# The page table as one 64-byte row per partition, pool_scale on GpSimd's queue, and the new tokens' pooling output kept in SBUF

## The chip, the cores and the metric

The kernel runs on one core of one Trainium2 chip. The metric is the device time of one execution in microseconds (us). An engine is called here by the name that the profile gives it: PE (TensorE's matmuls), PEld (its weight loads), DVE (VectorE), ACT (ScalarE), POOL (GpSimd) and SP (SyncE, which here only issues transfers). A `q` behind an engine's name means its instruction queue, where transfers are issued.

## The reference: what is computed

One step of a decoder layer for 1024 new prompt tokens and, for each of 8 samples, one new token behind 256 cached ones. All is float32.

```
p = rmsnorm(x) @ w_in          # split: q | cmp kv | slc kv | win kv | gates | za | u | zp
attn = gated sum of three branches (compressed blocks, selected blocks, window of 512)
pool = pool_mixer(u) * pool_scale          # 4 groups of 128 channels, windows 2, 4, 8, 16
y    = rmsnorm(x + concat(attn * silu(za), pool * silu(zp)) @ w_out)
cached keys and values of a sample: cache[page_table[sample]]     # 8 x 2 pages of 128 tokens
```

The page table has 8 x 2 int32 numbers, 64 bytes in all. `pool_scale` has 512 floats.

## The kernel before, in words

Every large product is made of three float32r products of high and low parts, so that each weight tile is first split: ACT copies the raw tile into a high part (`split_w`, L139), and DVE or POOL subtracts it for the low part (L140). The program runs in these stages.

1. The prompt's rows are normalised and transposed into `x` (chunks of 384 tokens), while the first token-major product (compressed keys and values, `cmp_unit`) already runs. SP loads `x_t` and the weights `w_raw`.
2. Two more token-major products, over selected and over window keys and values (loop over `br`, L302 to L339). A unit is 128 tokens: 24 matmuls (L244 to L246) into one of two PSUM banks, then on ACT a copy `kvf` (L314) and a copy into `V` (L316), on DVE the low part of `V` (L317). The keys are then transposed on PE (`kp`, L324). On PE the transpose of unit t stands behind the matmuls of unit t+1, and it reads `kvf` of unit t.
3. Queries, compression of keys and values (with cached pages fetched by indirect DMA through `idx`), pooling groups (`u`, `zp`), with the new tokens' attention (`decode`) in between.
4. Attention over the prompt in 32 units, with the `za` gates, the output weights and the output projection as filler.

Instruction order: inside stage 1 the order on ACT, DVE, PE and POOL is that of the code. From L301 on, the framework orders the instructions of each engine at build time, so a small change of the code can move other instructions too. Every engine then runs its list in order: an instruction that waits holds back all behind it on its engine.

The weights of stage 3 (`ws_raw`, `load_tile`, L348) have two buffers. The first of them, for the queries, are loaded and split during stage 2: SP issues them behind the last `w_raw`, and ACT's splits (L139) stand in ACT's list between the `kvf` copies of stage 2.

Three places are touched by the change.

- The page table: `pti` is loaded on SP by two DMAs, one for each half of the partitions. Each of 64 partitions takes 8 numbers with a stride of two, so 1024 runs of 4 bytes in all. POOL turns them into row indices (`ptf` L384, `idx` L386), which the indirect DMAs of stage 3 read.
```
for h in range(2):
    nc.sync.dma_start(pti[h * 64:(h + 1) * 64], dap(ptab, h, [[0, 64], [2, NB], [1, 1]]))
```
- `psc` (L669), `pool_scale` laid out with one channel per partition and four groups: 512 runs of 4 bytes, on SP's queue behind the last query weights; DVE halves it (L670). The pooling output (L812, L816) reads it.
- The pooling output `bb` goes to DRAM (`b_d`, L818) and comes back in stage 4 as `mb` (`split_m`, L966), one tile of tokens at a time. The ninth tile holds the 8 new tokens. It is `m8` in the output projection (L999).

Of the kernel before, what the change touches and what calls it, by code (L numbers as in the profile page):

```python
# [7 lines left out]
F32 = mybir.dt.float32  # L8
F32R = mybir.dt.float32r
I32 = mybir.dt.int32  # L10
# [11 lines left out]
NEG = -1.0e9  # L22
# pacing of the filling products: steps per block of attention (gate path, output), blocks added per unit,
# steps at the start, lag in products
NZ, NO, C0, OW, PLAG = 0.8, 0.5, 2, 12, 100
ZORD = ([(0, 0), (0, 1), (0, 2), (1, 0), (1, 1), (1, 2)]
        + [(pt, c) for c in range(3) for pt in (2, 3)])
# the rows of the output weights, by half of their columns, that take the place of each chunk of x
WROWS = [[(0, k) for k in (4, 5, 6, 7, 0, 1)], [(0, 2), (0, 3)] + [(1, k) for k in (4, 5, 6, 7)],
# [12 lines left out]
def hybrid_step_kernel(ctx, tc, xp, xs, ccmp, cslc, cwin, spool, ptab, norm_g, w_in, cmp_pe, cmp_w1,  # L42
# [33 lines left out]

    # DRAM scratch
    q_d = dram.tile([2, 512, T], F32, name="q_d")
# [3 lines left out]

    # constants
    ident = pers.tile([128, 128], F32, name="ident")
# [7 lines left out]
    def ptr_rms(pool, ssq, n, name):  # L92
        """(ssq / D + eps) ** -0.5 for a [n, 1] column."""
        st = pool.tile([128, 2], F32, name=name, tag="rms", bufs=4)
        nc.gpsimd.tensor_scalar(st[:n, 0:1], ssq, 1.0 / D, 1e-6, op0=OP.mult, op1=OP.add)
        nc.gpsimd.tensor_tensor(st[:n, 1:2], st[:n, 0:1], mhalf[:n], op=OP.pow)
        return st[:n, 1:2]

    # persistent data
    KT = pers.tile([128, 2, KLEN], F32R, name="KT")  # L100
# [3 lines left out]
    qs_t = pers.tile([128, 4, NB], F32, name="qs_t")  # L104
    as_t = pers.tile([128, 4, NB], F32, name="as_t")
    mslc = pers.tile([128, T], BF16, name="mslc")
    mwin = pers.tile([128, 640], BF16, name="mwin")
# [55 lines left out]
    load_x(3)  # L163
    nc.sync.dma_start(pe32, cmp_pe)
    def spread_g(h):
        """The norm's weights from the first partition to all."""
        cs = slice(h * 512, h * 512 + 512)
        p = ps_any()
        nc.tensor.matmul(p, ones, gb[0:1, cs], start=True, stop=True)
        if h:  # L170
            nc.scalar.activation(gb[:, cs], p, AF.Copy)
        else:
            nc.vector.tensor_copy(gb[:, cs], p)

    # masks
    nc.gpsimd.memset(mslc, 0.0)
# [10 lines left out]

    # normalised x, transposed, as high and low parts
    rss = {}
# [35 lines left out]

    # token-major projections: compressed, selected and window keys and values, gate logits
    def tok_unit(hi, lo, cn, t, mid=None):
# [112 lines left out]
    nc.gpsimd.dma_start(g_d[:, :], gates[:NB, 8, :])  # L340
    # a token before the end of the first compressed block has no compressed branch
    vgate = pers.tile([128, 24], F32, name="vgate")
# [27 lines left out]
    def silu2(out, src):  # L370
        """2 * silu(src)"""
        nc.scalar.activation(out, src, AF.Tanh, scale=0.5)
        nc.vector.scalar_tensor_tensor(out, out, 1.0, src, op0=OP.add, op1=OP.mult)

    # page indices: row of 2 tokens each
    pti = keep.tile([128, NB], I32, name="pti")
    for h in range(2):
        nc.sync.dma_start(pti[h * 64:(h + 1) * 64], dap(ptab, h, [[0, 64], [2, NB], [1, 1]]))
    pm = keep.tile([128, 1], F32, name="pm")
# [3 lines left out]
    ptf = keep.tile([128, NB], F32, name="ptf")  # L383
    nc.gpsimd.tensor_copy(ptf, pti)  # L384
    idx = pers.tile([128, NB], I32, name="idx")
    nc.gpsimd.tensor_scalar(idx, ptf, 64.0, pm, op0=OP.mult, op1=OP.add)  # L386

    # compressed keys and values, prompt and samples
    ces = ExitStack()
# [98 lines left out]

    # queries
    for pt in range(4):  # L490
# [18 lines left out]
    def decode():  # L509
        """One new token per sample."""  # L510
        dp = des.enter_context(tc.tile_pool(name="dp", bufs=1, reuse_waits="tile"))
        # queries, one column per head and sample; qx: high parts, then low parts, per sample
        qs = dp.tile([128, NB, 8], F32, name="qs")
# [6 lines left out]
        def diag(ap):  # L520
            """The columns of each sample's own heads in [b, 2, 64] columns: [p, b, h]."""
            return bass.AP(tensor=ap.tensor, offset=ap.offset, ap=[ap.ap[0], [136, NB], [1, 8]])
# [59 lines left out]
        for br in range(2):  # L582
# [6 lines left out]
            for b in range(0, NB, 2):  # L589
# [8 lines left out]
                for bb in range(2):  # L598
                    f = dp.tile([128, 512], F32, name="kvx", bufs=4)
                    if br == 0:  # L600
                        nc.gpsimd.indirect_dma_start(out=f, out_offset=None, in_=cslc,
                                                     in_offset=bass.IndirectOffsetOnAxis(
                                                         ap=idx[:, b + bb:b + bb + 1], axis=0))
                    else:
                        nc.gpsimd.dma_start(f, cwin[b + bb].rearrange("(p two) c -> p (two c)", two=2))
                    for par in range(2):
                        nc.tensor.transpose(p[:, (bb * 2 + par) * 128:(bb * 2 + par + 1) * 128],
                                            f[:, par * 256:par * 256 + 128], ident)
                    # high and low parts of the values
                    v = dp.tile([128, 2, 2, 128], F32R, name="vx", bufs=8)  # L610
                    fv = f.rearrange("p (two f c) -> p two f c", two=2, f=2)[:, :, 1]
                    nc.scalar.activation(v[:, :, 0], fv, AF.Copy)
                    nc.gpsimd.tensor_sub(v[:, :, 1], fv, r32(v[:, :, 0]))
                    vx.append(v)
# [52 lines left out]
    bb = pp.tile([128, TOK], F32, name="bb")  # L667
    psc = pp.tile([128, 4], F32, name="psc")
    nc.sync.dma_start(psc, pool_scale.rearrange("(g p) -> p g", p=128))  # L669
    nc.vector.tensor_scalar(psc, psc, 0.5, None, op0=OP.mult)  # L670
    spt = pp.tile([120, 512], F32, name="spt")
# [11 lines left out]

    # pooling group
    at = ctx.enter_context(tc.tile_pool(name="at", bufs=2, reuse_waits="tile"))
# [16 lines left out]
    def stage1(i, pr_):  # L702
        """Scores and softmax of a pair of heads for 128 queries; yields between matmul groups."""
        kv = pr_ // 2
# [6 lines left out]
        sm = at.tile([128, 2, 4, 3], F32, name="sm", bufs=3)  # L711
        # the first tile of a head: compressed 0:64, selected 64:64+n; the second: window 0:wn
        c_m = mc[:, 56 - 8 * i:120 - 8 * i]
# [47 lines left out]
    for g in range(4):  # L761
# [44 lines left out]
        for c in range(3):  # L806
# [7 lines left out]
            else:  # L814
                # the last on the engine that stores them
                nc.scalar.activation(bb[:, cs], p[:, :n], AF.Copy, scale=psc[:, g:g + 1])  # L816
                nc.gpsimd.tensor_mul(bb[:, cs], bb[:, cs], sz[:, cs])
        nc.gpsimd.dma_start(b_d[g], bb)  # L818
    tc.keep_in_program_order(nc.sync.dma_start(npool_p, utok[:15]))
    tc.keep_in_program_order(nc.sync.dma_start(npool_s[:, 14], utoks))  # L820
    pes.close()

    # attention over the prompt; the gate path, the new tokens and the output projection fill in
    zap = ctx.enter_context(tc.tile_pool(name="zap", bufs=1, reuse_waits="tile"))
# [4 lines left out]
    def stage2(i, pr_):  # L829
        """Transposes, products with the values and their sum; a list of steps."""  # L830
        kv = pr_ // 2
# [63 lines left out]

    # tiles of za that hold one factor of the gated output: the gate or the attention's output
    half_done = set()
# [38 lines left out]
    def load_wo(c):  # L936
        """Output weights in the place of x's chunk c, which is no longer needed."""
        rows = WROWS[c]
# [20 lines left out]
    def split_m(i, part):  # L959
        """High and low parts of four of the eight row blocks of the mixed output."""  # L960
        op = O_["p"]
        t0 = i * 128
        n = 128 if i < 8 else NB
        if part:
            src = O_["p"].tile([128, 4, 128], F32, name="mb")[:, :, :n]
            nc.sync.dma_start(src, b_d[:, :, t0:t0 + n].rearrange("g p t -> p g t"))  # L966
        else:
            src = za[:, :, t0:t0 + n]
# [70 lines left out]
    def filler():  # L1039
# [7 lines left out]
        for i in range(1, 7):  # L1047
# [3 lines left out]
            for half in range(2):  # L1051
                yield from out_half(i, half, st)
        # the last tile: the pooling part ahead of its attention
        tail["r"] = load_r(7)
# [21 lines left out]
    def after(a, b):  # L1076
        """Keeps a behind b in their engine's order."""
        tc.add_manual_dep(a, b.name, mybir.DependencyInfo(
            mybir.DependencyClass.NoSync, mybir.DependencyReason.DATA), reason="order")

    def paced_fill(k):
        """Steps of the filler, none ahead of the attention's products emitted so far."""
        ins = nc.cur_bb.bb.instructions
# [121 lines left out]
```

## Time and profile before

| what | value |
|---|---|
| time, median of 3 runs | 656.16 us (655.71 to 656.98) |
| span of the profiled execution, first to last instruction | 654.4 us |
| median less span | 1.8 us |
| PE busy | 627.6 us, 96% of the span |
| PEld / DVE / ACT / POOL busy | 89% / 65% / 55% / 41% |
| mean granted TensorE clock | 0.990 |

The profiled execution is known by its span; the time of a run has also what lies around the span, so the two differ by 1.8 us. A busy share is an average over all stages, so the places where PE stands still are to be looked for one by one. In views of waits a line reads "who waited, on which tile, for whom". In a timeline the columns are start, length, engine, line, operation, and in brackets the idle time before it and what ended it; `x2` means that several instructions are merged. In a table of windows each engine has its busy time in the window, then come the granted clock as a share of 2.4 GHz, the share of the DMA engines' time that is busy, and GB/s.

### The profile page before, as it was taken

Reading aid. Unit: us, or ns where it says so; the run is one execution under the profiler, and the core shown is the slowest. Engines: PE = TensorE matmul, PEld = TensorE weight load, DVE = VectorE, ACT = ScalarE, POOL = GpSimd, SP = SyncE. Lnnn points to the kernel's source line nnn. Section 1 sums busy time; section 2 is a strip of 40 time slices with the busy share of each in tenths; the row PEclk is TensorE's granted clock in tenths of the full one; section 3 lists DMA queues with packets and bytes.
Section 4 is the critical chain, followed back from the end, with each engine's and each line's share of the span. In section 5 each row is a group of like instructions: output and inputs, shape, how many; then the busy total and the mean of one; then the engine's idle time right before and its main releaser. Section 6 shows DMA issues by size and latency. Waiting matters only on the chain. (4 is left out here: it accounts for less than half of the span.)

```text
span 654.4 us, 12214 instructions
## 1 busy us (share of the span) xinstructions
PE 627.6 (96%) x4141; PEld 581.6 (89%) x4141; DVE 426.0 (65%) x1306; ACT 361.0 (55%) x930; POOL 266.8 (41%) x410
## 2 busy tenths in 40 slices
PE   6995999999999999999999899999999999999995
PEld 4995999999999999998999888788899999988984
DVE  5741234555526547575797998779888788877652
ACT  5652233444413234325788787767587677665641
POOL 5153001431207424104565666736454445454511
PEclk9997999999999999999999999999999999999999
DMA  8432302984524342243313437212022030101001
GB/s 274 147 100 56 102 16 76 310 274 118 162 72 135 84 142 70 94 132 98 97 33 98 130 113 238 86 34 82 32 83 97 18 97 18 65 17 66 18 34 64
DMA packets 65677, 65.14 MB, mean 100 GB/s; under 512 B 6423, under 2 KB 56927, under 8 KB 65575
## 3 DMA queue, kind: packets, MB, share of 16 engines
q1 hardware_dynamic: 55599, 44.53, 22.8%
q0 software_dynamic: 3968, 12.76, 6.0%
q10 hardware_dynamic: 6048, 7.08, 3.0%
q8 instruction: 33, 0.54, 0.3%
q14 instruction: 29, 0.24, 0.1%
HBM read 50.99 MB, written 15.68 MB: 102 GB/s over the span
## 5 line engine op out<-in xcount | busy, mean ns | idle before, releaser
L756 POOL TENSOR_SCALAR Ps<-Ps,sm,gates 128x64 f32<-128x64 f32 (+1 forms) x120 | 75.3, 639 | 111.1 <-DVE sm L752 77.3
L736 PE MATMUL S<-KT,qt 128*128 128x320 f32 (+10 forms) x400 | 98.3, 347 | 1.9 <-DVE sm L699 1.8
L859 DVE TENSOR_TENSOR pl<-tp,ph 128x512 fp32r<-128x512 f32 (+1 forms) x136 | 89.9, 670 | 13.5 <-ACT ph L858 12.4
L858 ACT ACTIVATE ph<-tp 128x512 fp32r<-128x512 f32 (+1 forms) x136 | 76.6, 579 | 35.2 <-PE tp L853 28.2
L365 PE MATMUL pa<-x,ws_hi 128*128 128x384 f32 (+1 forms) x288 | 93.6, 325 | 0.0
L366 PE MATMUL pa<-x,ws_hi 128*128 128x384 f32 (+1 forms) x288 | 92.8, 322 | 0.0
L367 PE MATMUL pa<-x,ws_lo 128*128 128x384 f32 (+1 forms) x288 | 92.6, 322 | 0.0
L750 ACT ACTIVATE Ps<-Ps,sm 128x64 f32<-128x64 f32 (+8 forms) x128 | 70.6, 554 | 28.2 <-DVE sm L748 26.7
L995 PE MATMUL pj<-wo,mh 128*128 128x512 f32 x256 | 82.6, 400 | 0.0
L871 PE MATMUL O<-pl,V 128*128 128x256 f32 x264 | 77.7, 311 | 1.0 <-DVE pl L859 0.9
L870 PE MATMUL O<-ph,V 128*128 128x256 f32 x264 | 74.2, 295 | 0.0
L736 PEld LDWEIGHTS S<-KT,qt 128*128 128x128 f32 x400 | 63.9, 189 | 8.8 <-DVE sm L699 2.8
L244 PE MATMUL pa<-w_hi,x 128*128 128x256 f32 (+1 forms) x192 | 57.7, 301 | 0.2 <-DVE V L317 0.2
L246 PE MATMUL pa<-w_hi,x 128*128 128x256 f32 (+1 forms) x192 | 56.9, 296 | 0.4 <-DVE x L217 0.4
L245 PE MATMUL pa<-w_lo,x 128*128 128x256 f32 (+1 forms) x192 | 56.1, 293 | 0.0
L366 PEld LDWEIGHTS pa<-x,ws_hi 128*128 128x128 f32 x288 | 54.2, 188 | 0.4 <-issue 0.2
L365 PEld LDWEIGHTS pa<-x,ws_hi 128*128 128x128 f32 x288 | 54.2, 188 | 0.3 <-DVE us L776 0.2
L367 PEld LDWEIGHTS pa<-x,ws_lo 128*128 128x128 f32 x288 | 54.1, 188 | 0.3
L871 PEld LDWEIGHTS O<-pl,V 128*128 128x128 f32 x264 | 49.7, 188 | 4.8 <-DVE pl L859 3.0
L870 PEld LDWEIGHTS O<-ph,V 128*128 128x128 f32 x264 | 49.9, 189 | 2.0 <-ACT ph L858 0.2
L995 PEld LDWEIGHTS pj<-wo,mh 128*128 128x128 f32 x256 | 45.1, 188 | 7.0 <-PE S L736 0.4
L995 PE MATMUL pj<-wo,ml 128*128 128x512 f32 x128 | 50.6, 395 | 0.1
(279 smaller groups left out, 1530.9 us busy)
## 6 DMA issues: line engine op xcount, KB each, us to landing
ws_raw<-in_w_in SPq DMA_DIRECT2D x32, 256.0 KB
qt<-q_d SPq DMA_DIRECT2D x64, 128.0 KB
x_t<-in_x_prompt SPq DMA_DIRECT2D x8, 512.0 KB
wo_raw<-in_w_out SPq DMA_DIRECT2D x8, 512.0 KB
r<-in_x_prompt SPq DMA_DIRECT2D x8, 512.0 KB
out<-r SPq DMA_DIRECT2D x7, 512.0 KB
q_d<-qhl ACTq DMA_DIRECT2D x8, 384.0 KB
out<-kvf ACTq DMA_DIRECT2D x5, 512.0 KB
```

Source lines behind the costliest of these rows:

```text
L244: nc.tensor.matmul(p[:n, :cn], xh[c][:, k, ts_], hi[:, k, :cn], start=k == 0, stop=False)
L365: nc.tensor.matmul(p[:, :n], hi[:, k, :], xh[c][:, k, :], start=k == 0, stop=False)
L366: nc.tensor.matmul(p[:, :n], hi[:, k, :], xl[c][:, k, :], start=False, stop=False)
L367: nc.tensor.matmul(p[:, :n], lo[:, k, :], xh[c][:, k, :], start=False, stop=k == 7)
L736: nc.tensor.matmul(S[:, :ln], qt[:, f, h, :], KT[:, kv, k0 + a:k0 + a + ln], start=f == 0, stop=f == 1)
L750: nc.scalar.activation(regs[br], regs[br], AF.Exp, bias=sm[:, hh, 1, br:br + 1], accum_out=sm[:, hh, 2, br:br + 1])
L756: nc.gpsimd.tensor_scalar(regs[br], regs[br], sm[:, hh, 3, br:br + 1], gsrc[:, k:k + 1], op0=OP.mult, op1=OP.mult)
L858: nc.scalar.activation(ph[:, :m], tp[:, :m], AF.Copy)
L859: nc.vector.tensor_sub(pl[:, :m], tp[:, :m], r32(ph[:, :m]))
L870: nc.tensor.matmul(O[:, :256], vv, ph[:, a * 256:(a + 1) * 256], start=False, stop=False)
L871: nc.tensor.matmul(O[:, :256], vv, pl[:, a * 256:(a + 1) * 256], start=False, stop=last)
L995: nc.tensor.matmul(p, a[:, k % 4, :], w, start=first and kk == 0, stop=last and kk == 2)
```

## The change

`ptr` replaces `pti`: the 64 bytes of the page table go to each of 128 partitions in one DMA, issued on SP behind `pe32` in the first loads. POOL picks the numbers out with two copies. `psc` is loaded on POOL's queue at the end of stage 2 and halved on POOL. POOL copies the last 8 columns of each pooling output into `bs_t`, and the ninth tile of the output projection reads that in place of `mb`; its load is gone. Comments are removed as well, which shifts the line numbers.

```
+    bs_t = pers.tile([128, 4, NB], F32, name="bs_t")
+    psc = pers.tile([128, 4], F32, name="psc")
...
     nc.sync.dma_start(pe32, cmp_pe)
+    ptr = keep.tile([128, NB, 2], I32, name="ptr")
+    nc.sync.dma_start(ptr.rearrange("p b h -> p (b h)"), bc_rows(ptab, 128, 2 * NB))
...
     nc.gpsimd.dma_start(g_d[:, :], gates[:NB, 8, :])
+    nc.gpsimd.dma_start(psc, pool_scale.rearrange("(g p) -> p g", p=128))
+    nc.gpsimd.tensor_scalar(psc, psc, 0.5, None, op0=OP.mult)
...
-    pti = keep.tile([128, NB], I32, name="pti")
-    for h in range(2):
-        nc.sync.dma_start(pti[h * 64:(h + 1) * 64], dap(ptab, h, [[0, 64], [2, NB], [1, 1]]))
...
-    nc.gpsimd.tensor_copy(ptf, pti)
+    for h in range(2):
+        rs = slice(h * 64, h * 64 + 64)
+        nc.gpsimd.tensor_copy(ptf[rs], ptr[rs, :, h])
...
-    psc = pp.tile([128, 4], F32, name="psc")
-    nc.sync.dma_start(psc, pool_scale.rearrange("(g p) -> p g", p=128))
-    nc.vector.tensor_scalar(psc, psc, 0.5, None, op0=OP.mult)
...
                 nc.gpsimd.tensor_mul(bb[:, cs], bb[:, cs], sz[:, cs])
+                nc.gpsimd.tensor_copy(bs_t[:, g, :], bb[:, T:])
...
-        if part:
-            src = O_["p"].tile([128, 4, 128], F32, name="mb")[:, :, :n]
+        if part and i == 8:
+            src = bs_t
+        elif part:
+            src = O_["p"].tile([128, 4, 128], F32, name="mb")
```

Three places of the order show what this moves. First SP's queue from the first loads to the first weights of stage 3, before:

```order
L164 DMA pe_106<-in_cmp_pe 32x128
L148 DMA w_raw<-in_w_in 128x2x256 x2
L135 DMA x_t<-in_x_prompt 128x1024
L148 DMA w_raw<-in_w_in 128x2x256 x2
L135 DMA x_t<-in_x_prompt 128x1024 x3
L135 DMA x_t<-in_x_sample 8x1024
L148 DMA w_raw<-in_w_in 128x2x280 x4
L378 DMA pti<-in_page_table 64x8x1 x2
L354 DMA ws_raw<-in_w_in 128x4x128 x6
```

and of the change:

```order
L166 DMA pe_108<-in_cmp_pe 32x128
L168 DMA ptr<-in_page_table 128x16
L150 DMA w_raw<-in_w_in 128x2x256 x2
L137 DMA x_t<-in_x_prompt 128x1024
L150 DMA w_raw<-in_w_in 128x2x256 x2
L137 DMA x_t<-in_x_prompt 128x1024 x3
L137 DMA x_t<-in_x_sample 8x1024
L150 DMA w_raw<-in_w_in 128x2x280 x4
L360 DMA ws_raw<-in_w_in 128x4x128 x6
```

The page table has gone from the place between `w_raw` and `ws_raw` to the place behind `pe`, ahead of the second weights of stage 1.

Second POOL's list at the passage from stage 1 to stage 2 (`w_lo` of 128x560 are the window weights' low parts), before:

```order
L265 DMA out<-knew_11_612 8x256
L381 IOTA pm 64x1 x2
L140 TENSOR_TENSOR w_lo<-w_raw,w_hi 128x560 x2
L384 CAST ptf<-pti 128x8
L140 TENSOR_TENSOR w_lo<-w_raw,w_hi 128x560 x2
L386 TENSOR_SCALAR idx<-ptf,pm 128x8
L333 DMA out<-knew_20_900 8x256
```

and of the change:

```order
L269 DMA out<-knew_11_616 8x256
L345 DMA psc<-in_pool_scale 128x4x1
L384 IOTA pm 64x1 x2
L389 CAST ptf<-ptr 64x8 x2
L142 TENSOR_TENSOR w_lo<-w_raw,w_hi 128x560
L391 TENSOR_SCALAR idx<-ptf,pm 128x8
L142 TENSOR_TENSOR w_lo<-w_raw,w_hi 128x560 x2
L346 TENSOR_SCALAR psc<-psc 128x4
L142 TENSOR_TENSOR w_lo<-w_raw,w_hi 128x560
L337 DMA out<-knew_20_904 8x256
```

The load of `psc` has come in at the head, and the last of four `w_lo` now stands behind the halving of `psc`, which reads that load.

Third PE's list in the first part of `decode`, where a score product (`dS`) of the new tokens stands between the matmuls of a pooling group (`pa`), before:

```order
L365 MATMUL pa<-x_89,ws_hi 128x384
L366 MATMUL pa<-x_89,ws_hi 128x384
L367 MATMUL pa<-x_89,ws_lo 128x384
L621 MATMUL dS<-kxh,qx 128x258
L607 MATMUL dkt<-ident,kvx 128x128 x4
L622 MATMUL dS<-kxl,qx 128x258
L621 MATMUL dS<-kxh,qx 128x258
L622 MATMUL dS<-kxl,qx 128x258
L607 MATMUL dkt<-ident,kvx 128x128 x4
```

and of the change:

```order
L371 MATMUL pa<-x_91,ws_hi 128x384
L626 MATMUL dS<-kxh,qx 128x258
L612 MATMUL dkt<-ident,kvx 128x128 x4
L372 MATMUL pa<-x_91,ws_hi 128x384
L373 MATMUL pa<-x_91,ws_lo 128x384
L371 MATMUL pa<-x_91,ws_hi 128x384
L612 MATMUL dkt<-ident,kvx 128x128 x2
L372 MATMUL pa<-x_91,ws_hi 128x384
L373 MATMUL pa<-x_91,ws_lo 128x384
L627 MATMUL dS<-kxl,qx 128x258
L626 MATMUL dS<-kxh,qx 128x258
L627 MATMUL dS<-kxl,qx 128x258
```

Between the first transposes `dkt` and this first `dS` there were 34 matmuls `pa`, and there are 27 now; the group that stood together is spread. The rest of `decode` and stage 4 have shifts of the same kind. Up to `decode` the lists of PE, ACT and DVE have the same rows as before.

## Rows read from the trace of the kernel before

**Rows 1.** The page's head: span, and busy time of TensorE's two parts.

```profile
span 654.4 us, 12214 instructions
...
PE 627.6 (96%) x4141; PEld 581.6 (89%) x4141; DVE 426.0 (65%) x1306; ACT 361.0 (55%) x930; POOL 266.8 (41%) x410
```

**Rows 2.** Waits of PE, whole span: total, times, longest, in us.

```profile
PE kp L324 <- ACT kvf L314: 7.0, 1, 7.0
```

**Rows 3.** Timeline of PE in stage 2, around that wait.

```profile
54.30 0.28 PE L246 MATMUL pa<-w_hi,x 128*128 128x256 f32 x1
61.52 0.47 PE L324 MATMUL kp<-ident,kvf 128*128 128x128 f32 x1 [6.95 <-ACT kvf L314]
...
62.56 0.41 PE L245 MATMUL pa<-w_lo,x 128*128 128x256 f32 x1
62.77 0.41 PE L246 MATMUL pa<-w_hi,x 128*128 128x256 f32 x1
...
67.64 0.28 PE L244 MATMUL pa<-w_hi,x 128*128 128x256 f32 x1
67.76 0.28 PE L245 MATMUL pa<-w_lo,x 128*128 128x256 f32 x1
```

**Rows 4.** Timeline of ACT over the same stretch.

```profile
60.57 0.63 ACT L139 ACTIVATE ws_hi<-ws_raw 128x512 fp32r<-128x512 f32 x1 [9.96 <-DMA ws_raw<-in_w_in]
61.10 0.37 ACT L314 ACTIVATE kvf<-pa 128x256 f32<-128x256 f32 x1
...
64.77 0.63 ACT L139 ACTIVATE ws_hi<-ws_raw 128x512 fp32r<-128x512 f32 x1 [1.00 <-DMA ws_raw<-in_w_in]
```

**Rows 5.** Timeline of SP's queue: issues, in several narrow windows.

```profile
46.99 0.37 SPq L148 DMA_DIRECT2D w_raw<-in_w_in  x1
47.41 1.41 SPq L378 DMA_DIRECT2D pti<-in_page_table  x2
...
48.86 0.62 SPq L354 DMA_DIRECT2D ws_raw<-in_w_in  x1
...
61.95 0.37 SPq L354 DMA_DIRECT2D ws_raw<-in_w_in  x1
```

**Rows 6.** Windows: busy times, then clock, DMA share and GB/s.

```profile
49.50:55.00 5.50, 5.07 (x43) 4.87 (x42) 0.29 (x1) 1.11 (x2) 1.62 (x2) 1.00 0.05 2
...
57.40:67.60 10.20, 5.90 (x26) 5.61 (x27) 2.49 (x6) 3.40 (x8) 3.60 (x4) 0.50 0.40 99
```

**Rows 7.** Timeline of POOL over the same stretch.

```profile
48.38 2.74 POOL L140 TENSOR_TENSOR w_lo<-w_raw,w_hi 128x560 fp32r<-128x560 f32 x2
59.83 0.19 POOL L384 CAST ptf<-pti 128x8 f32<-128x8 int32 x1 [8.71 <-DMA pti<-in_page_table]
```

**Rows 8.** Timeline of PE: the first matmul that reads the window weights' low part.

```profile
81.55 0.29 PE L245 MATMUL pa<-w_lo,x 128*128 128x280 f32 x1
```

**Rows 9.** Instructions of tile psc: min/median/max ns, first and last start in us.

```profile
L669 SPq DMA_DIRECT2D psc<-in_pool_scale x1: 498/498/498, 191.4 to 191.4; - x1
L670 DVE TENSOR_SCALAR psc<-psc x1: 170/170/170, 196.5 to 196.5; 128x4 f32<-128x4 f32 x1
```

**Rows 10.** Timelines of DVE and PE at the first score product of decode.

```profile
221.68 0.14 DVE L596 TENSOR_TENSOR kxl<-kn,kxh 128x4 fp32r<-128x4 f32 x1
...
224.61 0.34 PE L367 MATMUL pa<-x,ws_lo 128*128 128x384 f32 x1
224.78 0.28 PE L621 MATMUL dS<-kxh,qx 128*128 128x258 f32 x1
```

**Rows 11.** Timelines of POOL and PE: the ninth tile's low part and its first use.

```profile
418.14 0.26 POOL L973 TENSOR_TENSOR m<-mb,m 128x32 fp32r<-128x32 f32 x1
...
423.65 0.71 PE L999 MATMUL pj<-wo,m 128*40 128x512 f32 x2
```

**Rows 12.** Windows over the rest of the program.

```profile
68.00:280.00 212.00, 212.00 (x1421) 206.05 (x1420) 105.43 (x265) 76.52 (x180) 57.10 (x78) 1.00 0.42 128
280.00:420.00 140.00, 134.87 (x899) 123.16 (x898) 109.55 (x452) 100.61 (x315) 79.48 (x136) 1.00 0.38 115
```

## The prediction

> **What bounds the kernel now.** I read the page's head first: PE is busy 627.6 of 654.4 us [rows 1], so a change can only help where PE stands still, or where it runs slowly. The view of waits of PE says where it stands still: the longest is 7.0 us in one piece, for the transpose `kp`, which wants `kvf` from ACT [rows 2]. The timeline puts it at the end of the third unit of stage 2: the last matmul starts at 54.30, and the transpose at 61.52, after 6.95 us of nothing [rows 3]. The reader should follow this wait back, engine by engine.
>
> On ACT, `kvf` ran at 61.10, directly behind a split `ws_hi` at 60.57, and that split had held ACT for 9.96 us, since 50.61, for the transfer of `ws_raw` [rows 4]. So ACT had nothing wrong with it: a weight tile that nobody needs before stage 3 stands in its list ahead of a copy that PE needs now. On SP's queue that `ws_raw` was issued at 48.86, directly behind the two loads of the page table at 47.41 [rows 5]. From issue to use it took 60.57 - 48.86 = 11.7 us. A `ws_raw` of the same shape, issued at 61.95, was in use at 64.77, so 2.8 us is what such a load takes when nothing is ahead of it [rows 4, 5]. What was ahead: POOL's copy of the page table waited until 59.83 for its transfer [rows 7], which was 12.4 us after the issue, and in 49.50 to 55.00 the DMA engines were 0.05 busy and moved 2 GB/s [rows 6]. The 1024 runs of 4 bytes pass at one per 12.1 ns (12.4 us / 1024), and the weights stand behind them in the same queue.
>
> The stall has a second price. The granted clock was 0.50 (1.2 GHz) from 57.40 to 67.60, after PE had been idle for some 3 us [rows 6]. In this stretch matmuls of 256 columns follow each other by 0.21 us (62.56 to 62.77), and by 0.12 us afterwards (67.64 to 67.76) [rows 3].
>
> **The change part by part.** *The page table leaves the queue ahead of `ws_raw`.* In the change, SP issues the first `ws_raw` directly behind the last `w_raw`, issued at 46.99 and taking 0.37 us, so at about 47.4 in place of 48.86 [rows 5]. With the 2.8 us from above it is there at 50.2; if it first waits its turn behind the last `w_raw`, say 1 us more, at 51.2. ACT comes free at 50.61. PE wants the transpose right behind the matmul of 54.30, thus at about 54.4, and ahead of it ACT needs 0.63 us for the split and 0.37 us for `kvf`. So the split has to start by 53.4, and it starts between 50.6 and 51.2: more than 2 us to spare, and the 6.95 us are gone whole. What is late next? The following splits wait for reloads of the two buffers, each some 2.1 us behind the one before (of three splits in a row the first is at 60.57 and the third at 64.77 [rows 4]). From 51.2 on they fall at 53.3, 55.4 and 57.5; the units end at 54.4 and then every 24 x 0.12 = 2.9 us, at 57.3 and 60.2. Each `kvf` then comes a good microsecond ahead of the transpose that reads it, so no smaller stall takes the place.
>
> *The clock.* If PE does not stand still, the clock has no reason to fall there. PE worked from 61.52 to 67.6 at half of the clock, 6.1 us, which at full clock is 3.05 us. So 3.05 us come back. The Trainium skill (TensorE: Matmul & The Clock Gate, Terms) prices the throttle as throttled time times (1 - K/N); with the 10.2 us of the row this is an estimate of 5.1 us, and the sum would be 2 us lower, 644.6. I do not take it: for 4.1 of the 10.2 us PE was idle, and idle time is counted in the 6.95 already.
>
> *The new load `ptr`.* 128 runs of 64 bytes. At the pace of the old one (12.1 ns per run) it takes 1.5 us, and at best next to nothing. It stands on SP ahead of the selected branch's weights, whose splits stand in the code at the units t = 4 to 7 of stage 1, and it has its next reader on POOL at 48: I take 0. Without this cover it would cost 1.5 us.
>
> *`psc` on POOL's queue.* 512 runs of 4 bytes, now in flight from about 48 us, beside the first `ws_raw`. Before, it went out at 191.4 and DVE had it by 196.5 [rows 9], so at most 5.1 us; at the pace of the page table it is 512 x 12.1 ns = 6.2 us. Behind its halving on POOL stands the last `w_lo`. POOL starts the four `w_lo` at about 48.5, each 1.37 us (2.74 for two [rows 7]), and with `psc` there at 54.2 the last is done by 56. PE reads the first `w_lo` of that group at 81.55 [rows 8], or 71.5 once the stall is gone. So 15 us of cover: 0 on the path. Its other effect, on `ws_raw`, is a rival below. The removed halving on DVE (0.17 us) and the place on SP's queue in 191 us lie where PE is busy without a gap: from 68 to 280 it is busy 212.00 of 212.00 us [rows 12]. They are worth 0.
>
> *Pooling output kept on chip.* Four copies of 128 x 8 on POOL, about 0.2 us each by the copy of the page table (0.19, 128 x 8 [rows 7]), ahead of stores that are read only in stage 4. One load less on SP, and the ninth tile is split earlier. It was ready at 418.14 + 0.26 = 418.4 and PE used it at 423.65 [rows 11], so nobody waited for it: 0.
>
> *The new order.* The build moves rows from `decode` on. The first score product stands 34 matmuls behind its transposes before and 27 now; at 0.17 us each (224.61 to 224.78) that is 1.2 us less, while its operand was done at 221.82 and it ran at 224.78 [rows 10]: 2.9 us of slack, 1.7 left. Other groups have less between them, and I charge 0.5 us for small stalls in sum. In stage 4, from 280 to 420, PE idles 140.00 - 134.87 = 5.1 us [rows 12]; another order can give back or take part of it. I have no row that says which, and put plus or minus 2 us on it.
>
> **Sum.** 654.4 - 6.95 - 3.05 + 0.5 = 644.9 us of span; with 1.8 us around it, 646.7. Against the median of the runs, 656.16 - 9.5 = 646.66. I round to 646.6. All of stage 3 stands behind PE without a gap [rows 12], so what PE gains at 54 us moves everything behind it, and I carry the gain to the end.
>
> **Rivals.** *The small packets only change places.* `psc` has half of the page table's runs, and now travels beside `ws_raw`. For it: it is the same kind of transfer, at the very moment at which the old one did harm. By the Trainium skill (DMA: Bandwidth & Descriptors, Issuing engines are not separate DMA queues) transfers of all queues run on the same engines and interleave; no run here shows two such transfers side by side. Priced by rows: if `ws_raw` had to wait for all of `psc`, issued at 47.9, it would arrive 6.2 us later and 0.7 us on (as 60.57 behind 59.83), at 54.8. The split and `kvf` then end at 55.8, PE stands for 1.4 us and the clock holds, since PE idled longer than that before it fell. That is 648.0, inside my range. It costs the whole gain only if the 512 runs take over 12 us, against at most 5.1 us in rows 9. Partial losses of 3.5 us and more, from this or the new order, would end at 650 to 654.8.
>
> *The stall is not the page table's.* If ACT waited for `ws_raw` for a reason of its own (its buffer, or the load of the DMA engines), nothing changes: 656.2. Against it: 0.05 of DMA time busy in the wait, and 2.8 us for the same load later.
>
> *Slower: PE waits inside `decode`.* PE takes its rows in order, and eight groups of score products have been moved, four for each of two branches. If each wanted its operands 1.6 us later than PE arrives, 13 us would be added and the time is about 659. For this the slack of 1.7 us left at the first group would have to be minus 1.6 in all of them, so the chain of copies on ACT and DVE would have to be over 3 us slower than in rows 10; DVE is only half busy there (105 of 212 us). It decides from 1.25 us per group on, where the gain of 10 is eaten up.
>
> **How the numbers follow.** The stall gone and the clock kept, with order effects of up to 3 us either way: 82%, 643.5 to 649.5. Partly given back, 649.5 to 654.8: 9%. No change: 5%. Slower: 4%. A time 0.2% away (1.3 us) is about what a measurement of this kernel can tell from no change; so faster 0.91, within 0.2% 0.05, slower 0.04. The range for 8 in 10 is 643.5 to 650: below, the sum less the 3 us that another order in stage 4 may give; above, the sum with `psc`'s 1.4 us and 2 us of stalls from the order.
>
> **What would show it.** Right: no wait of PE on `kp` between 50 and 65 us, the clock at 1.00 through that stretch, ACT's first `ws_hi` at about 51, the first window matmul (81.55 before) near 71.5, and a later stage that is the same but 10 us earlier. `psc` would be seen harmless if POOL's halving runs by 56. Wrong: `ws_hi` still held by its transfer beyond 53.4 (then the small packets of `psc`, or something else on the way, are the cause); or the window matmul at 71.5 and the end at 650 or later, which would put the loss into `decode` or stage 4, seen as new waits of PE there.

## The result, and the profile after

| | kernel before | changed kernel |
|---|---|---|
| time, median of 4 runs each | 655.94 us (655.71 to 656.98) | 649.08 us (648.2 to 651.2) |
| span of the profiled execution | 654.4 us | 647.2 us |
| mean granted TensorE clock | 0.990 | 0.996 |

The ratio is 0.9893, with an interval of 0.9875 to 0.9912: 6.9 us faster. The forecast was 9.5 us faster, 646.6 us, with a range of 643.5 to 650. Measured once more beside other versions (e9 below), the changed kernel took 649.93 us against 656.38 (0.9895, 0.9874 to 0.9916), so the result stands.

First the page's head and the waits of PE after the change. They answer to [rows 1, 2]: the wait for `kp` is not in the list any more, and a wait for `dkt` has come in.

```profile
span 647.2 us, 12187 instructions
...
PE 625.6 (97%) x4141; PEld 580.5 (90%) x4141; DVE 425.3 (66%) x1305; ACT 360.5 (56%) x930; POOL 271.1 (42%) x417
```

```profile
PE S L738 <- DVE sm L701: 4.1, 6, 1.3
...
PE dkt L612 <- DMA kvx<-in_cache_slc_kv,idx: 1.0, 2, 0.6
```

The timeline of PE in stage 2, where [rows 3] had 6.95 us of nothing. The transpose starts 0.12 us behind the matmul ahead of it.

```profile
55.34 0.28 PE L250 MATMUL pa<-w_hi,x 128*128 128x256 f32 x1
55.46 0.27 PE L328 MATMUL kp<-ident,kvf 128*128 128x128 f32 x1
```

The timelines of SP's queue, ACT and POOL [rows 4, 5, 7]. The first `ws_raw` stands directly behind the last `w_raw`, and ACT's split waits 0.18 us for it in place of 9.96. The load of `psc` goes out at 48.96, early in stage 2, though its line stands at the end of that stage's code. POOL's halving of `psc` has no wait noted: its load had landed by the time POOL was there.

```profile
48.04 0.37 SPq L150 DMA_DIRECT2D w_raw<-in_w_in  x1
48.46 1.01 SPq L360 DMA_DIRECT2D ws_raw<-in_w_in  x2
```

```profile
51.94 0.63 ACT L141 ACTIVATE ws_hi<-ws_raw 128x512 fp32r<-128x512 f32 x1 [0.18 <-DMA ws_raw<-in_w_in]
52.73 0.38 ACT L318 ACTIVATE kvf<-pa 128x256 f32<-128x256 f32 x1 [0.15 <-PE pa L250]
```

```profile
48.96 0.84 POOL L345 DMA_DIRECT2D psc<-in_pool_scale  x1
...
55.51 0.66 POOL L346 TENSOR_SCALAR psc<-psc 128x4 f32<-128x4 f32 x1
56.15 1.39 POOL L142 TENSOR_TENSOR w_lo<-w_raw,w_hi 128x560 fp32r<-128x560 f32 x1
```

The windows of [rows 6] and the first of [rows 12] again. In 57.40 to 67.60 the clock is 1.00 and PE busy all the time. But 68 to 280 is no longer without a gap: 0.96 us are missing.

```profile
49.50:55.00 5.50, 5.50 (x49) 5.50 (x49) 2.69 (x4) 3.46 (x8) 5.27 (x9) 1.00 0.50 147
57.40:67.60 10.20, 10.20 (x88) 10.20 (x88) 3.55 (x7) 3.72 (x11) 0.14 (x1) 1.00 0.51 136
68.00:280.00 212.00, 211.04 (x1395) 204.37 (x1394) 108.16 (x275) 73.62 (x173) 59.99 (x81) 1.00 0.42 126
```

To see where the time went, I set marks on PE: the first and the last transpose `kp` (stage 2), the first `ut` and the last `yp` (the pooling groups with `decode` between them), and the last `pj` (the end of stage 4). The view of a tile's instructions gives the first and last start at the end of each row. Of the kernel before:

```profile
L324 PE MATMUL kp<-ident,kvf x16: 270/272/475, 51.5 to 109.4; 128*128 128x128 f32 x16
...
L770 PE MATMUL ut<-ident,u x4: 272/272/282, 194.1 to 280.8; 128*15 128x128 f32 x4
...
L809 PE MATMUL yp<-ws,pw x24: 386/484/590, 205.9 to 292.6; 128*128 128x384 f32 x16, 128*128 128x264 f32 x8
...
L995 PE MATMUL pj<-wo,ml x128: 387/393/499, 414.2 to 646.0; 128*128 128x512 f32 x128
```

And of the changed kernel:

```profile
L328 PE MATMUL kp<-ident,kvf x16: 270/272/275, 52.5 to 100.2; 128*128 128x128 f32 x16
...
L772 PE MATMUL ut<-ident,u x4: 272/272/273, 184.9 to 272.8; 128*15 128x128 f32 x4
...
L811 PE MATMUL yp<-ws,pw x24: 386/484/591, 196.6 to 284.6; 128*128 128x384 f32 x16, 128*128 128x264 f32 x8
...
L1000 PE MATMUL pj<-wo,ml x128: 387/392/487, 407.1 to 638.4; 128*128 128x512 f32 x128
```

Differences of these starts, for the two kernels and for every kernel of the experiments below, one profiled execution each:

| kernel | first `kp` at | stage 2: first to last `kp` | last `kp` to first `ut` | `decode`: first `ut` to last `yp` | stage 4: last `yp` to last `pj` |
|---|---|---|---|---|---|
| before | 51.5 | 57.9 | 84.7 | 98.5 | 353.4 |
| changed | 52.5 | 47.7 | 84.7 | 99.7 | 353.8 |
| changed, again (e9) | 52.6 | 47.7 | 84.9 | 99.6 | 355.0 |
| page table alone (e1) | 52.5 | 47.7 | 84.5 | 98.4 | 355.6 |
| `psc` and kept output (e2) | 51.5 | 58.2 | 84.7 | 99.5 | 353.7 |
| one-row load in the old place (e3) | 51.4 | 47.7 | 84.7 | 98.5 | 353.2 |
| old load in the early place (e4) | 57.7 | 47.8 | 84.9 | 98.5 | 355.4 |
| page table and `psc` (e5) | 52.6 | 47.8 | 84.9 | 99.7 | 353.5 |
| page table and kept output (e6) | 51.6 | 47.8 | 84.6 | 98.5 | 353.3 |
| the same again (e10) | 51.4 | 47.8 | 84.5 | 98.5 | 354.2 |
| `psc` on SP ahead of `ws_raw` (e7) | 51.6 | 47.8 | 84.8 | 99.7 | 355.0 |
| old load on POOL's queue (e8) | 52.6 | 54.0 | 85.2 | 98.5 | 354.8 |
| dummy, other addresses (e11) | 51.5 | 47.8 | 85.1 | 98.5 | 354.3 |
| dummy, half, same bytes (e12) | 51.6 | 52.0 | 84.9 | 98.5 | 354.2 |

So in the changed kernel stage 2 gives 10.2 us, and 1.0 are lost ahead of it, 1.2 in `decode` and 0.4 in stage 4. The column of `decode` has only two values, 98.4 to 98.5 and 99.5 to 99.7, and the second is found in those kernels that move `psc`. In the last column even two executions of one kernel differ (353.3 in e6, 354.2 in e10), so one execution says little there. The first column has two values too, about 51.5 and 52.5, apart from e4; neither the early `ptr` nor the move of `psc` goes with the second (e8 has neither and stands at 52.6, e10 and e7 have one each and stand at 51.4 and 51.6). More on both columns below.

### The profile page after: what moved, and what is told of

Same layout as the page of the kernel before. It is cut to its first block, busy times and chain, and to the rows that moved or that the text cites. A ratio compares the mean times of both kernels' runs of the same rounds, so it can differ in the third digit from the quotient of the medians.

```text
span 647.2 us, 12187 instructions
## 1 busy us (share of the span) xinstructions
PE 625.6 (97%) x4141; PEld 580.5 (90%) x4141; DVE 425.3 (66%) x1305; ACT 360.5 (56%) x930; POOL 271.1 (42%) x417
## 5 line engine op out<-in xcount | busy, mean ns | idle before, releaser
L862 DVE TENSOR_TENSOR pl<-tp,ph 128x512 fp32r<-128x512 f32 (+1 forms) x136 | 89.8, 669 | 12.1 <-ACT ph L861 11.1
L248 PE MATMUL pa<-w_hi,x 128*128 128x256 f32 (+1 forms) x192 | 57.0, 298 | 0.0
L250 PE MATMUL pa<-w_hi,x 128*128 128x256 f32 (+1 forms) x192 | 56.0, 292 | 0.2 <-DVE x L221 0.2
L758 POOL TENSOR_SCALAR Pw<-Pw,sm,gates 128x640 f32<-128x640 f32 (+4 forms) x64 | 50.4, 788 | 0.0
```

Of the source, the lines that this page charges most:

```text
L248: nc.tensor.matmul(p[:n, :cn], xh[c][:, k, ts_], hi[:, k, :cn], start=k == 0, stop=False)
L758: nc.gpsimd.tensor_scalar(regs[br], regs[br], sm[:, hh, 3, br:br + 1], gsrc[:, k:k + 1], op0=OP.mult, op1=OP.mult)
L862: nc.vector.tensor_sub(pl[:, :m], tp[:, :m], r32(ph[:, :m]))
```

## The experiments

### The two halves of the change (e1, e2)

e1 has the page table's part alone, e2 all but that.

```
e1:  + ptr = keep.tile([128, NB, 2], I32, name="ptr")      # behind pe32
     + nc.sync.dma_start(ptr.rearrange("p b h -> p (b h)"), bc_rows(ptab, 128, 2 * NB))
     - pti = ...; two loads of pti                         # ahead of ws_raw
e2:  + psc on POOL's queue, halved on POOL; - psc on SP, halved on DVE
     + bs_t, read by the ninth tile in place of mb
```

> Before, with the page table alone read as one 64-byte row per partition behind pe32; psc and the ninth tile as before. The lists of PE, DVE and ACT are then those of before, row for row. My theory (the table gives all of the gain, the rest of the change costs by its new order): no wait on kp, the PE marks behind stage 2 10.2 us earlier, decode with no new wait, and a span of 644.2 us (654.4 - 10.2) if the clock rises at 13 us as before, 645.3 if it rises at 18 us as in the change; time 646 to 647. Rival (decode loses whatever its order is, because PE now comes 10 us earlier to cached pages that do not come earlier, and the early load of the table holds up the start): the marks lose 1.3 us inside decode again, span 647, time 649.

> Before, with psc on POOL's queue and the ninth tile from bs_t, the page table as before. PE, DVE and ACT have the lists of the change, row for row. My theory (the new order costs 1.3 us in decode and 0.4 to 0.7 us behind it): the wait on kp stays at 7 us, and the time is 1.5 to 2 us above before, 657.5 to 658. Rival (the order costs nothing): the time of before within 0.7 us, 656.

e1 took 648.06 us (645.57 to 648.76), ratio 0.9849 (0.9829 to 0.987); e2 658.4 (657.73 to 660.85), ratio 1.0038 (1.0023 to 1.0054). So the page table's part has the whole gain, and the rest costs time. The time of e1 lies nearer to the rival's 649 than to my 646 to 647, but the rival's mark is missing: `decode` takes 98.4 us in e1, as before. What e1's profiled execution has more is in the first and the last column of the table. The waits of PE in e2:

```profile
PE kp L326 <- ACT kvf L316: 7.2, 1, 7.2
...
PE dkt L611 <- DMA kvx<-in_cache_slc_kv,idx: 0.8, 2, 0.5
```

The old stall is there whole, and beside it the new wait in `dkt`, which e1 does not have. In e2 PE comes to `decode` no earlier than before (194.4 us) and still loses time there; in e1 it comes 9.4 us earlier and loses none. So the loss goes with the order and not with the earlier arrival.

### Its form or its place? (e3, e4)

The page table was changed in two ways at once: fewer, longer runs, and an earlier issue. e3 issues the one-row form where `pti` stood; e4 issues the old form in the early place.

```
e3:  - pti = ...; two loads of pti
     + ptr = ...; one load of ptr          # same place, ahead of ws_raw
e4:  + pti = ...; two loads of pti         # behind pe32
     - pti = ...; two loads of pti
```

> Before, with the one-row form of the page table, but issued where pti stood, directly ahead of the first ws_raw. If the form counts (128 runs, at 12.1 ns each 1.5 us, within the 2 us to spare): no wait on kp, the time of the table's part alone within 1 us. If the place counts (any read of the same 64 bytes by all partitions holds up what is behind it): ws_hi starts several us after 53, and the wait on kp keeps 2 us or more; time 649 to 656.

> Before, with the old form of the page table (1024 runs of 4 bytes in two DMAs), but issued with the first loads behind pe32. If the place alone were enough: the time of the table's part alone, 646 to 647. If the runs hold SP's queue wherever they stand: 12.4 us of it from about 6 to 18 us, so the weights and x_t tiles issued behind it at 7.8 and 10.4 come up to 8 us later, PE waits in stage 1 for some of them, and 1 to 6 us of the gain are lost; time 647 to 653.

e3 took 646.34 us (ratio 0.9863, 0.9834 to 0.9891), e4 652.31 (0.993, 0.9913 to 0.9946). In e3 ACT got its weights in time from the old place:

```profile
51.82 0.63 ACT L139 ACTIVATE ws_hi<-ws_raw 128x512 fp32r<-128x512 f32 x1 [1.23 <-DMA ws_raw<-in_w_in]
```

In e4 stage 2 is as short as in the change, but stage 1 is now held up: ACT waits 4.27 us for the tokens `x_t` that stand behind `pti`, and PE for ACT and DVE. The first `kp` is 6.2 us later than before.

```profile
24.98 1.06 ACT L198 ACTIVATE junk<-x_t 128x1024 bf16<-128x1024 f32 x1 [4.27 <-DMA x_t<-in_x_prompt]
```

```profile
26.94 0.43 PE L247 MATMUL pa<-w_hi,x 128*128 128x256 f32 x1 [1.81 <-ACT x L219]
29.02 0.58 PE L249 MATMUL pa<-w_hi,x 128*128 128x256 f32 x1 [1.43 <-DVE x L220]
```

The form did it; the early place alone moves the harm.

### Who costs the time in decode? (e5, e6, e7)

e5 is the change without the kept pooling output, e6 the change without the move of `psc`. e7 has the early `ptr`, and loads `psc` on SP's queue exactly where `pti` stood: 512 runs of 4 bytes ahead of the first `ws_raw`.

```
e7:  + ptr as in the change
     - two loads of pti
     + nc.sync.dma_start(psc, pool_scale.rearrange("(g p) -> p g", p=128))   # in their place
     - psc = pp.tile(...); its load behind the query weights                 # DVE's halving stays
```

> The page table's part of the change and psc on POOL's queue, the ninth tile as before. Of PE's list only the stretch of decode moves, as in the change; stage 4 has the list of before. My theory (the order in decode costs 1.5 us, by two waits of PE on cached pages and some transposes that follow less closely): the marks lose 1.5 us between the first ut and the last yp and nothing behind it; span 645.4 us when the clock rises at 13 us and does not fall again (643.9 + 1.5), up to 2.6 us more in executions where it does otherwise; time some 1.5 us above the page table's part alone. Rival (the loss in the change comes from bs_t or from the tighter POOL list): the time of the page table's part alone.

> The page table's part and the ninth tile from bs_t, psc as before. Decode has the list of before on PE, stage 4 that of the change. My theory: nothing lost in decode, 0.4 to 0.7 us lost between the last yp and the end; span 644.4 us at the best clock, time about 0.5 us above the page table's part alone. Rival (bs_t's copies hold up POOL in decode): 1 us or more lost before the last yp.

> The page table's part, and psc's 512 runs of 4 bytes on SP's queue exactly where the page table stood, directly ahead of the first ws_raw. If every 4-byte run costs the 12.1 ns that the page table's did: 6.2 us of queue, ws_hi starts near 55 to 56, PE waits 1.5 to 2.5 us on kp. If those runs were slow for another reason than their size (all partitions read the same 64 bytes): ws_hi starts by 53 and PE does not wait there. The order in decode is the one that psc's move gives, so the time is that of e5 plus any stall.

e5 took 648.73 us (0.9867, 0.9849 to 0.9886), e6 646.28 (0.9842, 0.9817 to 0.9867), e7 648.66 (0.9858, 0.9838 to 0.9879). In the table `decode` is 1.2 us longer in e5 and e7, and unchanged in e6. So it is the move of `psc`, not the kept output. The 0.4 to 0.7 us that I expected of the kept output in stage 4 do not show in e6 (353.3 against 353.4). And it isn't POOL's queue or its halving there, since e7 has neither: what e5, e7 and the change have in common is that the load of `psc` has gone from its old place at 191 us and that its tile is made in another pool, and with it goes another order of PE in `decode`. The rows of the change show what this order does. First, the last issues of the cached keys `kvx` (the numbers behind the durations are the first and last start), before and after:

```profile
L601 POOL DMA_INDIRECT kvx<-in_cache_slc_kv,idx x8: 945/956/1419, 200.1 to 226.9; - x8
```

```profile
L606 POOL DMA_INDIRECT kvx<-in_cache_slc_kv,idx x8: 946/1056/1906, 191.0 to 218.0; - x8
...
DMA to landing us min/median/max: 2.9/3.3/3.8
```

And PE's transposes of the last of them, before and after:

```profile
230.69 0.38 PE L607 MATMUL dkt<-ident,kvx 128*128 128x128 f32 x2
...
232.52 0.38 PE L607 MATMUL dkt<-ident,kvx 128*128 128x128 f32 x2
```

```profile
220.07 0.41 PE L612 MATMUL dkt<-ident,kvx 128*128 128x128 f32 x2 [0.56 <-DMA kvx<-in_cache_slc_kv,idx]
...
221.61 0.44 PE L612 MATMUL dkt<-ident,kvx 128*128 128x128 f32 x2 [0.40 <-DMA kvx<-in_cache_slc_kv,idx]
```

PE is 9.2 us ahead of before when it comes to `decode` (194.1 to 184.9). The last load goes out 8.9 us earlier, almost the same; landing 3.3 us later, it is there at 221.3. But PE wants the two pairs at 219.51 and 221.21, which is 11.2 and 11.3 us earlier than before: two microseconds of matmuls that stood ahead of them now stand behind. So PE waits 0.96 us. Which of the two makes the build order `decode` so, the load that is gone or the other pool of its tile, was not tried.

### The old load on another queue (e8)

Only the queue is changed: `nc.sync.dma_start(pti ...)` becomes `nc.gpsimd.dma_start(pti ...)`. Nothing stands ahead of `ws_raw` on SP any more.

> Before, with the two old loads of the page table (1024 runs of 4 bytes) issued on POOL's queue instead of SP's, at the same time. PE, DVE and ACT have the lists of before. If the harm was standing in the same queue ahead of ws_raw: no wait on kp, span 643.9 to 646.5, time that of the page table's part alone. If the small runs hold up the DMA engines for whoever comes: ws_hi stays late by more than 3 us and PE waits, time 650 to 656.

It took 653.67 us (0.9949, 0.9931 to 0.9966). The first split had its weights in time, the second did not:

```profile
51.94 0.63 ACT L139 ACTIVATE ws_hi<-ws_raw 128x512 fp32r<-128x512 f32 x1 [0.17 <-DMA ws_raw<-in_w_in]
...
61.85 0.63 ACT L139 ACTIVATE ws_hi<-ws_raw 128x512 fp32r<-128x512 f32 x1 [8.53 <-DMA ws_raw<-in_w_in]
```

POOL's copy of `pti` got its data at 61.75, and the DMA queues in 49 to 63 us (packets, MB, share of 16 engines' time) show POOL's queue, q0, which carried this load and one small store, with 96 packets that took 39.7% of all engines' time, more than the 1840 packets of q1:

```profile
61.75 0.19 POOL L384 CAST ptf<-pti 128x8 f32<-128x8 int32 x1 [4.89 <-DMA pti<-in_page_table]
```

```profile
q0 software_dynamic: 96, 0.01, 39.7%
q1 hardware_dynamic: 1840, 1.07, 28.4%
```

The first `ws_raw` was issued at 48.52, half a microsecond ahead of this load at 49.02; the second went out at about the same time as the load. So this load holds up transfers of another queue as well. It is not the queue order alone.

### What makes that load slow? (e11, e12)

e7 had left a puzzle: 512 runs of 4 bytes passed almost unnoticed. Both of these kernels have the early `ptr`, and a dummy load that nobody reads in the old place. e11 has the same 2 x 64 x 8 numbers with a step of two, but each partition takes them from a piece of `x` of its own. e12 has one half of the old load, all from the same 64 bytes.

```
e11: + nc.sync.dma_start(dum[h * 64:(h + 1) * 64], dap(xp, h, [[16, 64], [2, NB], [1, 1]]))   # h = 0, 1
e12: + nc.sync.dma_start(dum[:64], dap(ptab, 0, [[0, 64], [2, NB], [1, 1]]))
```

> The page table comes as one row per partition, early; in the place where the old load stood there is a load of the same form, 2 x 64 partitions x 8 numbers of 4 bytes with a step of two, but from 64 different pieces of x instead of the same 64 bytes for all partitions. Nobody reads it. Theory (the old load was slow because all partitions read the same 64 bytes): it passes in 1 to 2 us, ws_hi is taken up by 53, PE does not wait for kp, and the time is within 1 us of the version with the early row alone (gain about 10 us of the span less clock events). Rival (1024 runs of 4 bytes with a step of two are slow from any address): ws_hi at about 60.5 and PE's wait for kp of 7 us are back, and the time is that of the kernel before.

> As the run before, but the load in the old place is one half of the old one: 64 partitions, 512 runs of 4 bytes with a step of two, all from the same 64 bytes. Nobody reads it. If runs from the same bytes pass at a steady 12.1 ns each, 512 take 6.2 us and the first ws_hi starts at about 54.3, 0.9 us after the last moment that PE's list allows: a wait for kp of about 1 us. If it is not the bytes but the number of runs (512 passed in 1 us when pool_scale stood there), ws_hi starts by 53 and PE does not wait.

The first split in e11, and in e12:

```profile
52.28 0.63 ACT L139 ACTIVATE ws_hi<-ws_raw 128x512 fp32r<-128x512 f32 x1 [1.50 <-DMA ws_raw<-in_w_in]
```

```profile
55.86 0.63 ACT L139 ACTIVATE ws_hi<-ws_raw 128x512 fp32r<-128x512 f32 x1 [5.08 <-DMA ws_raw<-in_w_in]
```

Set against the issue of the first `ws_raw` on SP, this is the whole series:

| ahead of `ws_raw` on SP | issued | used | apart |
|---|---|---|---|
| nothing (e6) | 47.53 | 50.96 | 3.4 us |
| 128 runs of 64 bytes, the same bytes (e3) | 47.91 | 51.82 | 3.9 us |
| 512 runs of 4 bytes, `pool_scale` (e7) | 48.01 | 52.30 | 4.3 us |
| 1024 runs of 4 bytes, other addresses (e11) | 48.81 | 52.28 | 3.5 us |
| 512 runs of 4 bytes, the same 64 bytes (e12) | 48.34 | 55.86 | 7.5 us |
| 1024 runs of 4 bytes, the same 64 bytes (before, [rows 4, 5]) | 48.86 | 60.57 | 11.7 us |

e11's PE has no wait for `kp`. The same number of runs of the same size costs next to nothing from many addresses, and 8 us from one. (Counted from the issue of what stands ahead, at 47.43 in e11 and 47.41 before, it is 4.9 against 13.2 us, which makes the same difference.) Between the last two rows 512 runs make 4.2 us, 8.2 ns each; 3.4 us plus 8.2 ns for each run gives 7.6 and 11.8 us, which is near both rows. The pace of 12.1 ns had the fixed part of the wait in it. Where the partitions read the same bytes, the number of runs counts, and e3's 128, of 64 bytes each, cost 0.5 us. e12's PE waited 2.08 us for `kp`, where I had put 1; its time was 650.78 us (0.9912), that of e11 649.04 (0.9885), of two executions each.

e12 shows the second price of a stall as well. Its stage 2 is 4.2 us longer than e11's, with a wait of 2.1 us. Behind that wait the granted clock fell here too: its mean is 0.86 in 50 to 60 us and 0.97 in 60 to 70, where the change has 1.00 throughout.

```profile
PE kp L326 <- ACT kvf L316: 2.1, 1, 2.1
```

```profile
50.00:60.00 10.00, 7.59 (x54) 7.19 (x53) 1.79 (x4) 2.81 (x8) 4.68 (x4) 0.86 0.34 86
60.00:70.00 10.00, 10.00 (x84) 10.00 (x84) 3.55 (x7) 3.87 (x10) 0.00 (x0) 0.97 0.48 137
```

### The change against itself without psc's move (e9, e10)

Both side by side on one chip, four executions each.

> The changed kernel once more, beside a version of it without the move of pool_scale. Theory (the move of pool_scale costs 1.3 to 1.5 us in decode, and the late clock of the profiled execution belonged to that execution, not to the kernel): a ratio of about 0.986 to 0.989 to the kernel before, about 2 us above the version without the move; the granted clock may rise at another time than 18 us in this profile; the waits of PE in dkt, about 1 us in sum, are there again. Rival (the loss was chance): the two versions within 0.5 us of each other, and no waits in dkt.

> The change without the move of pool_scale (page table and kept pooling output alone), the version that was shortest so far. Theory: a ratio of about 0.984, 646.3 us where the kernel before takes 656, and 1.5 to 2.5 us shorter than the changed kernel. Rival (it was chance): same time as the changed kernel.

The change took 649.93 us (649.15 to 650.37), the version without the move of `psc` 647.30 (646.83 to 647.95; ratio 0.9862, 0.9842 to 0.9882). They don't overlap, and the better one beats both kernels. The waits in `dkt` were there again in the change, 0.8 us in sum. The two profiled executions are 3.4 us of span apart, and by the table 1.1 of them are in `decode`, 1.2 ahead of stage 2 and 0.8 in stage 4. In the last two places the clock of the changed kernel was at half for a while: 17 matmuls in 15 to 18 us where e10 had 24. First its windows there and in stage 4, then e10's first:

```profile
15.00:18.00 3.00, 3.00 (x17) 3.00 (x16) 2.56 (x4) 2.13 (x4) 0.73 (x1) 0.53 0.65 177
...
405.00:407.00 2.00, 2.00 (x8) 1.81 (x8) 2.00 (x6) 2.00 (x7) 1.81 (x2) 0.50 0.70 191
```

```profile
15.00:18.00 3.00, 2.82 (x24) 2.62 (x23) 2.56 (x4) 2.40 (x5) 0.97 (x3) 1.00 0.80 262
```

So 1.1 to 1.2 us of the difference are shown to go with the new order. Of the versions with the one-row load, those that move `psc` have medians of 648.7 to 649.9 (the change twice, e5, e7), the others 646.3 to 648.1 (e1, e3, e6, e10); e11, with its dummy load, took 647.28 and 650.8 in its two executions. Whether the new order also makes such stretches of half clock likelier, or they fell so by chance, stays open.

## Why the prediction was right, and where it was off

**The stall and the clock: right, in mechanism and size.** `pti` held up `ws_raw`, this held ACT, ACT held `kvf`, and PE stood for it. The steps read as forecast: no wait for `kp`, split at 51.94 (51 forecast, and this execution came 1.0 us late to stage 2), clock 1.00 in stage 2, no smaller stall in its place. Stage 2 is 10.2 us shorter; 6.95 + 3.05 = 10.0 was forecast. By the formula of the Trainium skill (TensorE: Matmul & The Clock Gate, Terms) the estimate for stage 2 would have been 12 us, 6.95 + 5.1; the measured 10.2 sides with the rows, since PE was idle in part of the throttled time. The rival's remark that the clock holds through a wait of 1.4 us was not tried; it did not hold through e12's wait of 2.1.

**The first window matmul** came at 72.43, not 71.5, though 10.2 us were saved: 1.0 us had been lost ahead of stage 2. In that execution 18 matmuls ran from 13 to 18 us, in 3.73 us of busy time, where the kernel before had 28 in 3.43:

```profile
13.00:18.00 5.00, 3.73 (x18) 3.44 (x18) 4.56 (x5) 2.64 (x5) 2.26 (x3) 1.00 0.68 183
```

These matmuls took 0.21 us each, the pace that rows 3 have at half clock, although the clock of the window reads 1.00; in e9, with 17 matmuls there, it reads 0.50 to 0.58 from 15 to 18 us. The five executions whose first `kp` is at 52.5 or 52.6 (the change, e1, e5, e8, e9) have 17 or 18 matmuls in 13 to 18 us, and those at 51.4 to 51.6 have 25 to 28. No step of mine had this, and it isn't the early `ptr`: e6 and e10 have that load in the same place, and their first `kp` is at 51.6 and 51.4, as before. That it belongs to the execution is likely but not shown, since both profiled executions of the changed kernel have it.

**The term that was mis-sized is "I charge 0.5 us for small stalls in sum" for the new order.** The new order cost 1.0 to 1.2 us in `decode` in every kernel that moves `psc`, twice what I had put. I had looked at the score products' slack, which held; the wait came at the transposes, whose data arrive by DMA, and which I had not checked against their landing. The rival *slower: PE waits inside `decode`* named the right place with a far too high price: two waits of half a microsecond, not eight of 1.6.

**`psc` beside `ws_raw`: 0, as put.** The rival by which the small packets only change places did not come true: `ws_raw` was waited for 0.18 us. Even on SP, ahead of `ws_raw` (e7), the load of `psc` cost under 1 us. My pace of 12.1 ns per run was no property of small runs, so the 6.2 us that I worked out for `psc` from it were too much. The sum did not suffer, since I put `psc` at 0 for its cover, but 1.4 us of the range's upper end came from it. The rule cited there (the Trainium skill, DMA: Bandwidth & Descriptors, Issuing engines are not separate DMA queues), that transfers of all queues run on the same engines, is borne out by e8, where `pti` on POOL's queue held up SP's weights by 8.53 us. Interleaving did not protect them.

**`ptr` at 0, the kept output at 0:** right. e6, with both, has stages as short as any, and e3 shows that even ahead of `ws_raw` the 128 runs cost half a microsecond. The 2 us that I left open for stage 4 were not needed for the order of instructions: between e6 and e10, the same kernel, stage 4 differs by 0.9 us.

**The sum.** 10.2 gained, 1.2 lost in `decode`, 0.4 in stage 4 and 1.0 at the start make 7.6; behind the last `pj` another 0.4 go (8.8 us to the end against 8.4), and 7.2 of the span are seen. The 1.0 at the start was in no term, and the range held it and the rest of the loss in `decode` only because its upper end had room for `psc` and for other stalls; in this the range was lucky. The kernel without the move of `psc`, for which my sum without the 0.5 gives 646.2, took 646.28 and 647.30.

## What to carry to other kernels

Where many partitions read the same few numbers, load them as one contiguous row per partition and pick them apart on an engine: here 512 reads of the same 64 bytes cost 4.1 us and 1024 of them 8.3, and weights issued behind them on the same queue, or beside them on another, waited. A load whose own reader is in no hurry can still make the longest stall of a kernel, so follow a wait through the engine to the queue and look at what stands ahead there. And when a small change lets a scheduler reorder another stage, check each moved instruction that reads a transfer against its landing; here an edit with no work in it gave back a tenth of the gain.

## What the runs showed of the hardware

- 1024 runs of 4 bytes from 64 different pieces of DRAM put the next transfer back by 1.4 us at most (4.85 us in e11, from the issue of the runs, less the 3.43 of e6; part of it is the issuing), the same runs from one piece of 64 bytes by 8 us more. Why the chip does so was not tried.
- From POOL's queue the same load keeps the DMA engines busy, from SP's it does not: a share of 1.15 in 49.50 to 55.00 in e8, against 0.05 before [rows 6] and 0.50 in the change, where the weights move without it. Both hold up the weights; stage 2 lost 6.2 us in e8 (54.0 against 47.8) and 10.1 before.
- The same kernel's executions differ by short stretches of half clock. In e1 one lay in stage 4, at 291 to 294; stage 4 took 355.6 us there against 353.2 in e3, which runs the same order and has no such stretch:

```profile
291.00:294.00 3.00, 2.98 (x9) 3.00 (x10) 1.15 (x12) 2.83 (x16) 2.22 (x6) 0.50 0.46 133
```

  The five longest stages 4 of the table (354.8 to 355.6) are those of e1, e4, e7, e8 and e9, and only their traces show such a stretch in it. Three of these kernels have the old order in `decode` and two the new one, too few to tell whether the order has a part.

  e1's five executions spread from 645.57 to 648.76 us, so differences under some 2 us need several executions, or the marks of one stage, as used here for `decode`.
